# More gathered tokens, a turned value product and a float32 retrieval table in an encoder layer with a product-key expert block

## The chip, the cores and the metric

The kernel runs on one core of one Trainium2 chip. The metric is the device time of one execution in microseconds (us), the median of the runs. PE is TensorE, DVE is VectorE, ACT is ScalarE, POOL is GpSimd, SP is SyncE, which here only issues DMAs.

## What is computed

One encoder layer on 512 tokens of width 2048 in float32. Its last part, the expert block, is what changes:

```python
q = (xt @ w_query).reshape(t, P_HEADS, 2, P_HALF)
s = jnp.einsum('thcd,hcnd->thcn', q, sub_keys)
sv, si = lax.top_k(s, P_TOPK)
cand = sv[:, :, 0, :, None] + sv[:, :, 1, None, :]
cidx = si[:, :, 0, :, None] * N_KEYS + si[:, :, 1, None, :]
top_s, top_j = lax.top_k(cand.reshape(t, P_HEADS, P_TOPK * P_TOPK), P_TOPK)
idx = jnp.take_along_axis(cidx..., top_j, axis=-1)
g = jax.nn.softmax(top_s, axis=-1)
ue = jnp.take(expert_u, idx, axis=0)
ve = jnp.take(expert_v, idx, axis=0)
act = jax.nn.gelu(jnp.einsum('td,thkd->thk', xt, ue), approximate=False) * g
out = h + jnp.einsum('thk,thkd->td', act, ve)
```

There are 16384 experts (128 x 128 keys), 8 heads and 16 experts a head, so each token uses 128 (expert, weight) slots. `expert_u` and `expert_v` are 128 MiB each.

## The kernel before

Float32 products are made of float32r parts: each operand is split into a high and a low part, and `mm3` issues three matmuls (high x high, high x low, low x high) into one PSUM bank. A common stream of 1 MiB weight granules feeds all products: `take` at granule i makes the high part of granule i+2 on ACT (`whi`, L104), the low part of i+1 on DVE (`wlo`, L109) and has SP fetch granule i+4 (`raw`, L89). There are three buffers of each.

The expert block handles tokens in two ways. The 128 tokens of block 0 **gather**: slot by slot, an indirect DMA of POOL fetches 128 rows of 8 KB (one a token), and DVE makes a dot product (L912, with `expert_u`) or adds a weighted row (L1014, with `expert_v`). The other 384 tokens (`SD`) go **dense** over all 16384 experts, in two stages of 128 steps each.

Score stage (`score`): a step takes 128 experts, 16 slices of 128 rows, 48 matmuls of 384 moving tokens with `expert_u` as the stationary side. ACT applies Gelu and writes the 128 x 384 scores to DRAM (`s_d`). Beside it run, in portions that `Paced` hands out four times a step, the choice of experts (`choose`, on DVE, for four blocks of 128 tokens), the gather's dot products, and the **retrieval table**: for each dense token a 128 x 128 matrix of weights over its experts, the product of two one-hot matrices over the 128 slots. `rb` is made by two ACT instructions (L863, L864), `ra` by one on DVE (L872) with high and low part of the weight side by side, one float32r matmul of 256 columns (L847) multiplies them, ACT copies the high half of two tokens (L851) and DVE adds the low half (L856). Sixteen tokens make a `gs` tile, written to `g_d`.

Value stage: in a step i, 256 experts by 1024 output columns; chunks of 8 steps share 1024 experts (4 steps for one half of the columns, 4 for the other). `weigh` multiplies the stored scores with the stored table (L986, in place in `st`) and splits the product into `ath` (ACT, L121) and `atl` (DVE, L122). These are the stationary side; the expert granule moves, 512 columns a matmul, 36 matmuls a step, into 6 of 8 PSUM banks, which DVE adds to `acc` (L1051) after each half chunk. SP loads the table of the next chunk (`gt`, 1.5 MiB) and the scores (`st`); each `st` load is issued one step ahead of its use:

```python
            if j % 2 == 0:
                load_scores(ck + 1, j // 2)
            else:
                weigh(ck + 1, j // 2)
```

Every engine works its instructions in order, so one that waits holds up all behind it.

Of the kernel before, what the change touches and what calls it, by code (L numbers as in the profile page):

```python
# [16 lines left out]
P = 128  # L17
S = 512
D = 2048
# [9 lines left out]
G0 = P  # L29
SD = S - G0  # L30
FH = 258
# [4 lines left out]
def tile_encoder_layer(ctx: ExitStack, tc: tile.TileContext, x, g1, g2, qkg, sg, lv, nd, cs, cc,  # L36
# [18 lines left out]
    g_d = dram.tile([SD // GT, P, NE, GT], F32, name="g_d")  # L55
# [149 lines left out]
    sgs, qkgs, rstd0, lam = few[:, 5:7], few[:, 7:9], few[:, 9:10], few[:, 10:11]  # L205
    idx0 = const.tile([P, P], U32, name="idx0")
    w0 = const.tile([P, P], F32, name="w0")
    dots = const.tile([P, P], F32, name="dots")
    qks = few[:, 11:11 + HEADS + 1]
# [441 lines left out]
    with ExitStack() as st:  # L651
# [32 lines left out]
        nc.vector.tensor_copy(rstd0, rstd[0])  # L684
# [85 lines left out]
    def choose(tb):  # L770
# [58 lines left out]
        if tb == 0:  # L829
            nc.vector.scalar_tensor_tensor(idx0, abf[:, 0].rearrange("p h k -> p (h k)"), float(NE),  # L830
                                           abf[:, 1].rearrange("p h k -> p (h k)"), op0=ALU.mult, op1=ALU.add)
            return
        yield 0.5
        sel = vals[0].rearrange("p (a b) k -> p a (b k)", a=2)
        selw = idxs[0].bitcast(F32R).rearrange("p (a b) k -> p a (b k)", a=2)
# [6 lines left out]
        split(ps[:, 2 * P:3 * P], selw[:, 0], selw[:, 1])  # L842
        late, sums, rbs = [], [], {}

        def place():
            gs, ps, t, ra, rb = late.pop(0)
            nc.tensor.matmul(ps[:, t % 2], rb, ra.rearrange("p a b -> p (a b)"), start=True, stop=True)  # L847
            if t % 2:
                t0 = t % GT - 1
                pair = gs[:, :, t0:t0 + 2].rearrange("p i t -> p t i")  # L850
                nc.scalar.copy(pair, ps[:, :, :P])  # L851
                sums.append((gs, ps, t, pair))

        def add():
            gs, ps, t, pair = sums.pop(0)
            nc.vector.tensor_add(pair, ps[:, :, P:], pair)  # L856
            if t % GT == GT - 1:
                nc.scalar.dma_start(g_d[((tb - 1) * P + t) // GT], gs)

        for t in range(-2, P):  # L860
            if t + 2 < P:
                rbs[t + 2] = rb = pool.tile([P, P], F32R, name="rb", bufs=6)
                nc.scalar.activation(rb, iota, AF.Abs, bias=sel[:, 1, t + 2:t + 3], scale=-1.0)  # L863
                nc.scalar.activation(rb, f32(rb), AF.Relu, bias=unit, scale=-1.0)  # L864
            if t < 0:
                continue
            if t % GT == 0:
                gs = gpool.tile([P, NE, GT], F32, name="gs")
            if t % 2 == 0:
                ps = bank("tr").rearrange("p (t a) -> p t a", t=2)  # L870
            ra = pool.tile([P, 2, P], F32R, name="ra", bufs=4)
            nc.vector.scalar_tensor_tensor(ra, iota[:, None, :].to_broadcast([P, 2, P]), sel[:, 0, t:t + 1],  # L872
                                           f32(selw[:, :, t:t + 1]).to_broadcast([P, 2, P]),
                                           op0=ALU.is_equal, op1=ALU.mult)
            late.append((gs, ps, t, ra, rbs.pop(t)))
            if t % 2:
                if sums:
                    add()
# [5 lines left out]
        while sums:  # L884
            add()

    def begin():
        gb = big.tile([P, D], F32, name="b8")
        nc.scalar.dma_start(hn0, h_d[0])
        nc.scalar.dma_start(gb, bass.AP(tensor=g2r.tensor, offset=g2r.offset, ap=[[0, P], [1, D]]))  # L890
        yield from choose(0)
        nc.vector.scalar_tensor_tensor(hn0, hn0, rstd0, gb, op0=ALU.mult, op1=ALU.mult)
# [5 lines left out]
    def gather_dots():  # L898
        rows = {}

        def fetch_row(s):
            if s < P:
                rows[s] = big.tile([P, D], F32, name="b8")
                nc.gpsimd.indirect_dma_start(out=rows[s], out_offset=None, in_=eu,
                                             in_offset=bass.IndirectOffsetOnAxis(ap=idx0[:, s:s + 1], axis=0))
# [3 lines left out]
        for s in range(P):  # L909
            fetch_row(s + 2)  # L910
            row = rows.pop(s)
            nc.vector.scalar_tensor_tensor(row, row, 1.0, hn0, op0=ALU.mult, op1=ALU.mult,  # L912
                                           accum_out=dots[:, s:s + 1])
# [15 lines left out]
    E0, LAST = 7, NE - 6  # L929
    begin, others = Paced(begin(), 30.5), Paced(others(), 3 * (33.5 + 64 * 1.0))  # L930
    gather = Paced(gather_dots(), float(P))
# [33 lines left out]
    nc.scalar.activation(dots, dots, AF.Gelu)  # L965
    nc.vector.tensor_mul(w0, w0, dots)
    pg.close()
    p6.close()

    pool = pool_of(ctx, "p7")  # L970
    gts, sts, ats = {}, {}, {}

    def load_weights(ck):
        gts[ck] = pool.tile([P, SD // GT, R, GT], F32, name="gt")
        nc.sync.dma_start(gts[ck], g_d[:, :, ck * R:(ck + 1) * R, :].rearrange("c p i t -> p c i t"))

    def load_scores(ck, e2):
        i0 = ck * R + 2 * e2
        sts[ck, e2] = pool.tile([P, 2, SD], F32, name="st", bufs=2)
        nc.sync.dma_start(sts[ck, e2], s_d[i0:i0 + 2].rearrange("e p t -> p e t"))  # L980

    def weigh(ck, e2):
        st = sts.pop((ck, e2))
        for ee in range(2):
            sv = st[:, ee, :].rearrange("p (c t) -> p c t", t=GT)
            nc.vector.tensor_mul(sv, sv, gts[ck][:, :, 2 * e2 + ee, :])  # L986
        h = pool.tile([P, 2, SD], F32R, name=f"ath{e2}", bufs=2)
        l = pool.tile([P, 2, SD], F32R, name=f"atl{e2}", bufs=2)
        split(st, h, l)
        ats[ck, e2] = (h, l)  # L990

    load_weights(0)
    for e in range(LAST, NE):
        score(e, pool, None)
        if e - LAST < R // 2:
            load_scores(0, e - LAST)
        if 0 < e - LAST <= R // 2:
            weigh(0, e - LAST - 1)
# [154 lines left out]
```

## Time and profile before

| | us |
|---|---|
| median of 3 runs (3970.6 to 3976.12) | 3971.14 |
| the profiled execution | 3967.92 |
| its span | 3966.2 |
| score stage, 1751.2 to 2868.9 of the span | 1117.7 |
| value stage, 2868.9 to 3962.2 | 1093.3 |
| from the end of the value stage to the end of the span | 4.0 |

The stages' bounds are the starts of their first matmuls, and the start and end of the last. Starts in a timeline are what sets the pace of PE: its matmuls overlap, so the duration of one is longer than the distance to the next.

### The profile page before, as it was taken

The page shows a single profiled execution, that of the slowest core. Times are in us where ns is not written, and L with a number is a line of the kernel's source. Part 1 is how long each engine was busy: PE and PEld are TensorE (multiplying, and loading weights), DVE is VectorE, ACT ScalarE, POOL GpSimd, SP SyncE. Part 2 cuts the span into 40 slices and gives each one's busy share as a digit, 9 for nine tenths or more (in the row PEclk, how much of TensorE's full clock was granted, in tenths as well). Part 3 has the DMA queues.
Part 4 walks back from the last instruction along what each step waited for, and adds up shares of the span by engine and source line. Part 5 has one row for each costly group of instructions (what it writes and reads, how often), then busy time and mean ns, then how long its engine had stood idle before and what let it go on. Part 6 is the DMA issues. An engine that isn't in the chain of part 4 may idle for free.

```text
span 3966.2 us, 49642 instructions
## 1 busy us (share of the span) xinstructions
PE 3904.3 (98%) x20143; PEld 3459.1 (87%) x20143; DVE 2642.2 (67%) x3884; ACT 1501.0 (38%) x2120; POOL 504.5 (13%) x339
## 2 busy tenths in 40 slices
PE   8999999999999999999999999999999999999999
PEld 6888898888888888889999999999978788787777
DVE  5534555556423424689999888989567787777875
ACT  4322323333322222233675477378422222222221
POOL 0000111111000000001111211211022222222221
PEclk9999999999999999999999999999999999999999
DMA  4334122222333333237888788878788788787885
GB/s 159 112 133 146 64 96 80 80 80 80 107 122 133 135 121 125 98 123 266 299 310 299 286 314 304 307 288 318 245 306 312 283 308 310 286 306 292 310 298 194
DMA packets 209229, 836.65 MB, mean 211 GB/s; under 512 B 15292, under 2 KB 97244, under 8 KB 134876
## 3 DMA queue, kind: packets, MB, share of 16 engines
q1 hardware_dynamic: 147136, 498.11, 35.1%
q0 software_dynamic: 36992, 268.47, 18.1%
q10 hardware_dynamic: 24872, 66.89, 4.4%
q8 instruction: 159, 2.61, 0.3%
q14 instruction: 70, 0.57, 0.0%
HBM read 766.30 MB, written 67.11 MB: 210 GB/s over the span
## 4 chain that ended last, share of the span: by engine, by line
PE 74%; DVE 10%; DMA 8%; issue 5%; ACT 1%; POOL 0%; SPq 0%; DVEq 0%; ACTq 0%; POOLq 0%
PE mm L131 20%; PE mm L133 20%; PE mm L132 20%; DMA st<-s_d 8%; DVE wlo L109 4%; DVE acc L1014 3%; PE vb L132 3%; PE vb L133 3%; PE vb L131 2%; DVE acc L1051 2%; DVE st L986 1%; PE tr L131 1%; PE tr L132 1%; PE tr L133 1%; ACT ath L121 1%
## 5 line engine op out<-in xcount | busy, mean ns | idle before, releaser
L104 ACT CAST whi<-raw 128x2048 fp32r<-128x2048 f32 x395 | 753.8, 1911 | 1004.0 <-PE vb L133 373.1
L131 PE MATMUL mm<-ah,whi 128*128 128x384 f32 (+1 forms) x3072 | 1087.6, 354 | 0.0
L132 PE MATMUL mm<-al,whi 128*128 128x384 f32 (+1 forms) x3072 | 1083.7, 353 | 0.0
L133 PE MATMUL mm<-ah,wlo 128*128 128x384 f32 (+1 forms) x3072 | 1083.6, 353 | 0.0
L109 DVE TENSOR_TENSOR wlo<-raw,whi 128x2048 fp32r<-128x2048 f32 x395 | 901.5, 2285 | 264.0 <-ACT whi L104 264.0
L132 PE MATMUL vb<-wlo,ath 128*128 128x512 f32 x1536 | 602.7, 392 | 33.0 <-DVE wlo L109 33.0
L133 PEld LDWEIGHTS mm<-ah,wlo 128*128 128x128 f32 x3072 | 577.3, 188 | 40.2
L131 PEld LDWEIGHTS mm<-ah,whi 128*128 128x128 f32 x3072 | 577.7, 188 | 39.1 <-issue 0.2
L132 PEld LDWEIGHTS mm<-al,whi 128*128 128x128 f32 x3072 | 577.5, 188 | 39.1
L131 PE MATMUL vb<-whi,ath 128*128 128x512 f32 x1536 | 601.0, 391 | 2.7 <-DVE acc L1051 2.7
L133 PE MATMUL vb<-whi,atl 128*128 128x512 f32 x1536 | 600.8, 391 | 0.0
L131 PE MATMUL mm<-whi,ah 128*128 128x512 f32 (+1 forms) x1408 | 501.8, 356 | 2.9 <-ACT ah L121 2.9
L133 PE MATMUL mm<-whi,al 128*128 128x512 f32 (+1 forms) x1408 | 496.3, 352 | 0.0
L132 PE MATMUL mm<-wlo,ah 128*128 128x512 f32 (+1 forms) x1408 | 495.6, 352 | 0.0
L132 PEld LDWEIGHTS vb<-wlo,ath 128*128 128x128 f32 x1536 | 290.2, 189 | 99.0 <-DVE wlo L109 38.9
L1012 POOL DMA_INDIRECT row<-in_ev_dram,idx x128 | 252.7, 1974 | 859.3 <-DVE acc L1014 743.7
L131 PEld LDWEIGHTS vb<-whi,ath 128*128 128x128 f32 x1536 | 290.2, 189 | 64.7 <-DVE acc L1051 3.9
L133 PEld LDWEIGHTS vb<-whi,atl 128*128 128x128 f32 x1536 | 290.4, 189 | 60.2
L912 DVE SCALAR_TENSOR_TENSOR b<-b,hn 128x2048 f32<-128x2048 f32 x128 | 292.0, 2287 | 13.5 <-DMA b<-in_eu_dram,idx 13.5
L1014 DVE SCALAR_TENSOR_TENSOR acc<-row,w,acc 128x2048 f32<-128x2048 f32 x128 | 300.1, 2344 | 0.3
L133 PEld LDWEIGHTS mm<-whi,al 128*128 128x128 f32 x1408 | 267.2, 190 | 37.3 <-DVE al L122 0.7
L131 PEld LDWEIGHTS mm<-whi,ah 128*128 128x128 f32 x1408 | 267.5, 190 | 36.4 <-ACT ah L121 3.6
(303 smaller groups left out, 3506.0 us busy)
## 6 DMA issues: line engine op xcount, KB each, us to landing
raw<-in_up_dram SPq DMA_DIRECT2D x128, 1024.0 KB, 5.6
raw<-in_ev_dram SPq DMA_DIRECT2D x128, 1024.0 KB, 7.8
raw<-in_wqkv_dram SPq DMA_DIRECT2D x48, 1024.0 KB, 4.8
s_d<-ge ACTq DMA_DIRECT2D x128, 192.0 KB, 4.6
g_d<-gs ACTq DMA_DIRECT2D x24, 1024.0 KB, 9.0
gt<-g_d SPq DMA_DIRECT2D x16, 1536.0 KB, 15.8
st<-s_d SPq DMA_DIRECT2D x64, 384.0 KB, 7.2
raw<-in_wgf_dram SPq DMA_DIRECT2D x16, 1024.0 KB, 4.8
```

The lines of the kernel that those rows point to most:

```text
L104: nc.scalar.copy(his[i], raws[i])
L109: nc.vector.tensor_sub(los[i], raws.pop(i), f32(his[i]))
L121: nc.scalar.copy(hi, src)
L131: nc.tensor.matmul(ps, ah, bh, start=first, stop=False, skip_group_check=shared)
L132: nc.tensor.matmul(ps, ah, bl, start=False, stop=False, skip_group_check=shared)
L133: nc.tensor.matmul(ps, al, bh, start=False, stop=last, skip_group_check=shared)
L912: nc.vector.scalar_tensor_tensor(row, row, 1.0, hn0, op0=ALU.mult, op1=ALU.mult, accum_out=dots[:, s:s + 1])
L986: nc.vector.tensor_mul(sv, sv, gts[ck][:, :, 2 * e2 + ee, :])
L1012: nc.gpsimd.indirect_dma_start(out=row, out_offset=None, in_=ev, in_offset=bass.IndirectOffsetOnAxis(ap=idx1[:, s:s + 1], axis=0))
L1014: nc.vector.scalar_tensor_tensor(acc[0], row, w0[:, s:s + 1], acc[0], op0=ALU.mult, op1=ALU.add)
L1051: nc.vector.tensor_add(acc[tb + 1][:, ds_], banks[tb * 2 + dc], acc[tb + 1][:, ds_])
```

## The change

A second group of tokens is gathered: the first 32 of block 1 (`G2`), so that 160 tokens gather and `SD` is 352. One instruction serves four slots of each of the 32 tokens (4 x 32 partitions), so 32 more indirect DMAs and 32 more DVE instructions in each gather. Their normed rows are read four times from DRAM (`hn_d`), multiplied with the gain and parked in `hg_d`. The table's matmul is float32 with 128 columns, without the split; ACT copies four tokens at a time. `g_d` is laid out by chunk, so that it is written in pieces of 512 B and read contiguously. In the value stage the expert granule is the stationary side and the 352 tokens move; 8 banks fill and are added to a turned sum `accT`. Scores are loaded three uses ahead. After the last step the sums are turned back, added to h (loaded there) and written.

```diff
+G2 = 32
+Q = P // G2
+G0 = P + G2
 SD = S - G0
...
-    g_d = dram.tile([SD // GT, P, NE, GT], F32, name="g_d")
+    g_d = dram.tile([P, NE // R, NG, R, GT], F32, name="g_d")
...
         def place():
             gs, ps, t, ra, rb = late.pop(0)
-            nc.tensor.matmul(ps[:, t % 2], rb, ra.rearrange("p a b -> p (a b)"), start=True, stop=True)
-            if t % 2:
...
-                nc.scalar.copy(pair, ps[:, :, :P])
+            nc.tensor.matmul(ps[:, t % 4], rb, ra, start=True, stop=True)
+            if t % 4 == 3:
+                at = t % GT - 3
+                nc.scalar.copy(gs[:, :, at:at + 4].rearrange("p i t -> p t i"), ps)
...
-            nc.vector.tensor_add(pair, ps[:, :, P:], pair)
...
-            ra = pool.tile([P, 2, P], F32R, name="ra", bufs=4)
-            nc.vector.scalar_tensor_tensor(ra, iota[:, None, :].to_broadcast([P, 2, P]), sel[:, 0, t:t + 1],
+            ra = pool.tile([P, P], F32, name="ra", bufs=5)
+            nc.vector.tensor_scalar(ra, iota, sel[:, 0, t:t + 1], selw[:, t:t + 1],
...
             if t % 2:
...
-                yield 1.0
+                yield 0.5
...
+        nc.vector.tensor_mul(hn0, hn0, gb)
+        hb = big.tile([P, D], F32, name="b8")
+        for r in range(Q):
+            nc.scalar.dma_start(hb[r * G2:(r + 1) * G2], hn_d[P:G0])
+        nc.vector.tensor_mul(hb, hb, gb)
+        nc.scalar.dma_start(hg_d, hb)
...
-    begin, others = Paced(begin(), 30.5), Paced(others(), 3 * (33.5 + 64 * 1.0))
-    gather = Paced(gather_dots(), float(P))
+    begin, others = Paced(begin(), 30.5), Paced(others(), 3 * 33.5 + SD * 0.25)
+    gather = Paced(gather_dots(), P + G2 + 1.0)
...
+    def load_scores(n):
+        if n < len(pairs):
+            sts[n] = pool.tile([P, 2, SD], F32, name="st", bufs=3)
+            nc.sync.dma_start(sts[n], s_d[2 * n:2 * n + 2].rearrange("e p t -> p e t"))
...
+    nc.sync.dma_start(acc0, h_d[0])
+    nc.gpsimd.memset(acc2, 0.0)
...
+    def add_up(ck, half, dt, ps):
+        dst = accT[:, half * 8 + dt, :]
+        if ck == 0:
+            nc.scalar.copy(dst, ps)
+        else:
+            nc.vector.tensor_add(dst, ps, dst)
...
+    shares = [0.8, 0.8, 1.3, 1.0, 1.3, 1.3, 0.8, 0.7]
+    given, total = 0.0, sum(shares) * (NE // R) - 6.0
+    owed, first_use = [], {step_of(n): n for n in range(len(pairs))}
     for i in range(NE):
...
         vh, vl = take(2)
...
+        for job in owed:
+            add_up(*job)
...
+        for dt in range(8):
+            ds_ = slice(dt * P, dt * P + P)
...
+            for ee in range(2):
+                mm3(banks[dt], (vh[:, ee, ds_], vl[:, ee, ds_]), (h[:, ee, :], l[:, ee, :]),
+                    e2 == 0 and ee == 0, e2 == R // 2 - 1 and ee == 1)
+        n = first_use.get(i + 2)
+        if n is not None:
+            weigh(n)
+            load_scores(n + 3)
+        if j == 2 and ck > 0:
+            load_weights(ck + 1)
+        given += shares[j]
+        gather.to(given / total)
+        if e2 == R // 2 - 1:
+            for dt in range(4):
+                add_up(ck, half, dt, banks[dt])
+            owed = [(ck, half, dt, banks[dt]) for dt in range(4, 8)]
...
+    for t0, n in ((P, G2), (G0, P), (G0 + P, P), (G0 + 2 * P, SD - 2 * P)):
+        row = accp.tile([P, D], F32, name="row", bufs=3)
+        nc.sync.dma_start(row[:n], rows_d[t0:t0 + n])
+        for dc in range(4):
...
+            if t0 < G0:
+                nc.tensor.matmul(ps[:n], some, acc2[:, ds_], start=True, stop=True)
             else:
+                for k in range(4):
+                    nc.tensor.transpose(ps[:n, k * P:(k + 1) * P], accT[:, dc * 4 + k, t0 - G0:t0 - G0 + n], ident)
+            nc.vector.tensor_add(row[:n, ds_], ps[:n], row[:n, ds_])
+            nc.sync.dma_start(out[t0:t0 + n, ds_], row[:n, ds_])
```

Three places show how instructions move. First SP's queue in a middle chunk of the value stage, before:

```order
L975 DMA gt<-g_d 128x24x128
L980 DMA st<-s_d 128x2x384
L89 DMA raw<-in_ev_dram 128x2x1024 x2
L980 DMA st<-s_d 128x2x384
L89 DMA raw<-in_ev_dram 128x2x1024 x2
L980 DMA st<-s_d 128x2x384
```

and SP's queue there after the change:

```order
L94 DMA raw<-in_ev_dram 128x2x1024
L1005 DMA gt<-g_d 128x2816
L94 DMA raw<-in_ev_dram 128x2x1024 x4
L1010 DMA st<-s_d 128x2x352
L94 DMA raw<-in_ev_dram 128x2x1024
L1010 DMA st<-s_d 128x2x352
```

The loads are the same in kind, but an `st` load now serves the third use after it, three to seven steps later, where it served the next step.

Second DVE's order around the end of a half chunk in the value stage, before:

```order
L1014 SCALAR_TENSOR_TENSOR acc_24303<-row,w_87,acc_24303 128x2048
L986 TENSOR_TENSOR st<-st,gt 128x384 x2
L122 TENSOR_TENSOR atl_27022<-st,ath_27021 128x768
L1051 TENSOR_TENSOR acc_24304<-vb,acc_24304 128x512 x2
L1051 TENSOR_TENSOR acc_24305<-vb,acc_24305 128x512 x2
L1051 TENSOR_TENSOR acc_24306<-vb,acc_24306 128x512 x2
L109 TENSOR_TENSOR wlo<-raw,whi 128x2048
```

and DVE there after the change:

```order
L1058 SCALAR_TENSOR_TENSOR acc_23814<-row,w_89,acc_23814 128x2048 x2
L1068 TENSOR_TENSOR accT<-vb,accT 128x352 x4
L114 TENSOR_TENSOR wlo<-raw,whi 128x2048
L1068 TENSOR_TENSOR accT<-vb,accT 128x352 x4
L1058 SCALAR_TENSOR_TENSOR acc_23814<-row,w_89,acc_23814 128x2048
```

The half's sums are added in two groups of four with a `wlo` between them, and `weigh` no longer stands at this place in every half.

Third SP's queue at the end of the program, before:

```order
L89 DMA raw<-in_ev_dram 128x2x1024 x5
L1016 DMA out_dram<-acc_24303 128x2048
L1053 DMA out_dram<-acc_24304 128x512 x2
L1053 DMA out_dram<-acc_24305 128x512 x2
L1053 DMA out_dram<-acc_24306 128x512 x2
```

and SP's queue there after the change:

```order
L94 DMA raw<-in_ev_dram 128x2x1024 x5
L1112 DMA row<-h_d 32x2048
L1122 DMA out_dram<-row 32x512 x4
L1112 DMA row<-h_d 128x2048
L1122 DMA out_dram<-row 128x512 x4
L1112 DMA row<-h_d 128x2048
L1122 DMA out_dram<-row 128x512 x4
L1112 DMA row<-h_d 96x2048
L1122 DMA out_dram<-row 96x512 x4
```

Before, only writes stood at the end; now loads of h stand between the writes, each behind the four writes of the tile ahead.

## Rows read from the trace of the kernel before

**Rows 1.** Stage by stage: busy time (instructions) of each engine, granted clock, DMA.
```profile
core 0: us, PE busy (x) PEld busy (x) DVE busy (x) ACT busy (x) POOL busy (x), PEclk, DMA share, GB/s
...
1922.00:2140.50 218.50, 218.24 (x1297) 217.61 (x1296) 196.68 (x265) 171.94 (x357) 31.49 (x28) 1.00 0.83 303
2140.50:2251.00 110.50, 110.50 (x640) 110.47 (x640) 101.30 (x189) 39.12 (x43) 19.06 (x15) 1.00 0.83 300
...
2868.90:3962.20 1093.30, 1057.60 (x4609) 869.13 (x4607) 800.52 (x626) 287.70 (x187) 252.70 (x128) 0.99 0.80 293
```

**Rows 2.** The same view of three stretches without a stall: 256, 384, 512 moving columns.
```profile
409.50:432.50 23.00, 23.00 (x193) 23.00 (x192) 9.13 (x17) 4.88 (x4) 3.99 (x2) 1.00 0.26 93
1809.50:1892.70 83.20, 83.20 (x482) 83.20 (x481) 73.76 (x153) 26.94 (x23) 12.98 (x11) 1.00 0.81 294
2982.50:3031.40 48.90, 48.90 (x217) 40.52 (x216) 32.84 (x26) 13.80 (x9) 11.56 (x6) 1.00 0.84 309
```

**Rows 3.** Who waited for whom in the value stage: us, times, longest.
```profile
DVE st L986 <- DMA st<-s_d: 199.1, 29, 12.3
...
DVE atl L122 <- ACT ath L121: 54.3, 60, 1.1
...
PE vb L132 <- DVE wlo L109: 33.0, 14, 5.7
```

**Rows 4.** PE's timeline at a key match (float32) and at a table product.
```profile
1608.97 1.05 PE L726 MATMUL tr<-b,qT 128*128 128x128 f32 x8
1609.78 0.48 PE L131 MATMUL mm<-ah,whi 128*128 128x512 f32 x1
1610.10 0.40 PE L132 MATMUL mm<-al,whi 128*128 128x512 f32 x1
...
2095.49 0.40 PE L847 MATMUL tr<-ra,rb 128*128 128x256 f32 x2
2095.72 0.34 PE L131 MATMUL mm<-ah,whi 128*128 128x384 f32 x1
```

**Rows 5.** ACT's timeline while the table is made.
```profile
2098.01 0.49 ACT L937 ACTIVATE ge<-mm 128x384 f32<-128x384 f32 x1 [1.29 <-PE mm L133]
2098.53 0.34 ACTq L938 DMA_DIRECT2D s_d<-ge  x1
2098.91 1.92 ACT L104 CAST whi<-raw 128x2048 fp32r<-128x2048 f32 x1 [0.41 <-ACT ge L937]
2100.72 0.40 ACT L863 ACTIVATE rb<-iota,vals 128x128 fp32r<-128x128 f32 x1
...
2102.19 0.58 ACT L851 COPY gs<-tr 128x256 f32<-128x256 f32 x1
2102.57 0.38 ACT L863 ACTIVATE rb<-iota,vals 128x128 fp32r<-128x128 f32 x1
```

**Rows 6.** The chain that ended last, in a stretch of the value stage: start, us, what.
```profile
3045.49 2.47 DVE acc L1051 x4
...
3052.43 2.20 DVE wlo L109
3054.63 2.26 DVE acc L1014
3056.89 0.95 DVE st L986 x2
...
3057.86 0.85 ACT ath L121
```

**Rows 7.** The gathered rows of the value stage: issues, additions, time to landing.
```profile
L1012 POOL DMA_INDIRECT row<-in_ev_dram,idx x128: 939/1897/2933, 2887.4 to 3902.5; - x128
...
DMA to landing us min/median/max: 7.4/10.1/13.4
```

**Rows 8.** DVE's timeline: the last addition; DMA issues of the page, with us to landing.
```profile
3962.39 0.69 DVE L1051 TENSOR_TENSOR acc<-vb,acc 128x512 f32<-128x512 f32 x1 [0.67 <-PE vb L133]
...
raw<-in_wga_dram SPq DMA_DIRECT2D x16, 1024.0 KB, 4.8
```

**Rows 9.** DMA rate in 40 slices of the two stages, score and value.
```profile
GB/s 208 169 299 272 301 334 260 311 299 320 294 323 285 330 284 315 292 318 228 327 294 303 320 289 315 307 310 290 325 249 320 274 306 355 315 252 369 249 265 163
...
GB/s 334 303 328 289 344 235 303 325 297 342 233 302 323 278 339 297 283 316 299 333 268 268 296 277 345 314 270 312 293 330 295 284 318 286 342 269 285 276 234 39
```

**Rows 10.** Weight loads of the value stage: busy us, mean ns of one.
```profile
L132 PEld LDWEIGHTS vb<-wlo,ath 128*128 128x128 f32 x1536 | 290.2, 189 | 99.0 <-DVE wlo L109 38.9
```

More of the change, by code (lines that the diff above doesn't have):

```diff
@@ L28 @@
 GT = 16
-G0 = P
+G2 = 32
+Q = P // G2
+G0 = P + G2
 SD = S - G0
+NG = SD // GT
 FH = 258
@@ L54, in tile_encoder_layer @@
     s_d = dram.tile([NE, P, SD], F32, name="s_d")
-    g_d = dram.tile([SD // GT, P, NE, GT], F32, name="g_d")
+    g_d = dram.tile([P, NE // R, NG, R, GT], F32, name="g_d")
+    hn_d = dram.tile([G0, D], F32, name="hn_d")
+    hg_d = dram.tile([P, D], F32, name="hg_d")
     def bank(tag):
@@ L208, in tile_encoder_layer @@
     dots = const.tile([P, P], F32, name="dots")
+    iw2 = const.tile([P, 2, G2], U32, name="iw2")
+    idx2, w2 = iw2[:, 0], f32(iw2[:, 1])
+    dots2 = const.tile([P, G2], F32, name="dots2")
     qks = few[:, 11:11 + HEADS + 1]
@@ L1022, in tile_encoder_layer @@
         vh, vl = take(2)
-        if i < 4:
-            tb = (i + 1) % NT
-            nc.sync.dma_start(acc[tb], h_d[tb])
+        for job in owed:
+            add_up(*job)
+        owed = []
         if e2 == 0:
-            banks = [vps.tile([P, 512], F32, name="vb") for _ in range(6)]
-        h, l = ats[ck, e2]
-        for tb in range(3):
-            ts_ = slice(tb * P, (tb + 1) * P)
-            for dc in range(2):
-                ds_ = slice(dc * 512, dc * 512 + 512)
-                for ee in range(2):
-                    mm3(banks[tb * 2 + dc], (h[:, ee, ts_], l[:, ee, ts_]), (vh[:, ee, ds_], vl[:, ee, ds_]),
-                        e2 == 0 and ee == 0, e2 == R // 2 - 1 and ee == 1)
@@ L1036, in tile_encoder_layer @@
-        if i == 2:
-            nc.vector.tensor_copy(idx1, idx0)
-        if i >= 4:
-            gather.to((i - 3) / (NE - 8))
-        if ck + 1 < NE // R:
-            if j == 0:
-                load_weights(ck + 1)
-            if j % 2 == 0:
-                load_scores(ck + 1, j // 2)
-            else:
-                weigh(ck + 1, j // 2)
-        if e2 == R // 2 - 1:
-            for tb in range(3):
-                for dc in range(2):
-                    ds_ = slice(half * 1024 + dc * 512, half * 1024 + dc * 512 + 512)
-                    nc.vector.tensor_add(acc[tb + 1][:, ds_], banks[tb * 2 + dc], acc[tb + 1][:, ds_])
-                    if ck == NE // R - 1:
-                        nc.sync.dma_start(out[(tb + 1) * P:(tb + 2) * P, ds_], acc[tb + 1][:, ds_])
@@ L1054, in tile_encoder_layer @@
-    gather.to(1.0)
+            banks = []
+        h, l = ats[ck * 4 + e2]
+        for dt in range(8):
+            ds_ = slice(dt * P, dt * P + P)
+            if e2 == 0:
+                banks.append(vps.tile([P, 512], F32, name="vb")[:, :SD])
+            for ee in range(2):
[5 more added lines that the diff above has]
+            load_scores(n + 3)
@@ new lines, in tile_encoder_layer @@
+        if j == 2 and ck > 0:
[6 more added lines that the diff above has]
+            owed = [(ck, half, dt, banks[dt]) for dt in range(4, 8)]
+    gather.to(1.0)
+    rows_d = h_d.rearrange("n p d -> (n p) d")
+    some = pool.tile([P, G2], F32, name="some")
+    nc.vector.tensor_reduce(some, ident.rearrange("p (r t) -> p t r", r=Q), axis=AX.X, op=ALU.add)
```

146 lines of the change are left out of this document (85 added, 61 removed).

## The prediction

> **What bounds the kernel now.** I read the stages first. In both stages of the expert block PE is busy nearly all the time, at full clock, and DVE for 73 to 92% of it [rows 1]. A busy PE is not yet a PE at its pace, so next I looked at stretches where nothing waits: 192 matmuls of 256 columns take 23.0 us, 480 of 384 take 83.2, 216 of 512 take 48.9 [rows 2]: 119.8, 173.3 and 226.4 ns from start to start. The steps are 53.5 and 53.1 ns for 128 columns, so a matmul costs 0.416 ns a column and some 13 ns that don't depend on its width. At this pace the score stage's 6144 matmuls need 1064.9 us and its 192 pairs of table products 44 (0.23 a pair, [rows 4]); the stage takes 1117.7, so 9 us are stall. The value stage's 4608 matmuls need 1043 of 1093, so 50 are stall. The waits name the cause: PE waits for `wlo`, and DVE, which makes it, stood 199 us waiting for `st` and 54 for ACT's `ath` [rows 3]. With its 800.5 us of work [rows 1] that fills 1054 of 1093 us: DVE has no room to be late. Ahead of the score stage the change only adds 1.25 MB of writes of the normed rows; the query products run on beside them, and without that cover they would cost one transfer, about 5 us [rows 8].
>
> **The change, part by part.**
>
> *Score matmuls.* 352 instead of 384 columns: 173.3 - 32 x 0.416 = 160.0 ns, 6144 times: **-81.9 us**. 256 and 384 columns stand on either side, so little is open.
>
> *Value matmuls.* 48 a step instead of 36, each of 352 columns: 6144 x 160.0 = 983.0 instead of 1043: **-60**. The turned product pays 13 ns a third more often, and wins by 384 against 352 dense tokens.
>
> Against this speaks a rule of the Trainium skill ("Perfetto Trace Analysis", section "Identifying the Most-Contended Engine"): matmul busy time misleads, and the summed time of the weight loads is the better measure of how near TensorE is to its limit. Here it would go from 4608 x 189 ns [rows 10] = 871 us to 6144 x 189 = 1161, more than the stage has now. The trace does not bear it out as a bound: in the stretch of 256 columns 192 loads, 36 us at 189 ns, fit in 23.0 us [rows 2, 10]. As a mechanism it stands among the rivals.
>
> *Table.* Four float32 matmuls of a key match show as eight records [rows 4]. From their start to that of the second matmul behind them pass 1.13 us, of which an ordinary 0.23 is not theirs: 0.90, or 0.226 a matmul and 0.45 a pair. 176 pairs make 79 us, where 192 made 44: **+35**. DVE loses its additions and half of each `ra`.
>
> ACT is close behind. Between table steps it spends 1.47 us on the four activations of a pair (2100.72 to 2102.19) and 0.38 on a copy of 256 columns [rows 5]. The copy of 512 is not in the trace: 0.38 plus 256 columns at 1.82/2048 = 0.61 at least, twice its busy 0.58 at most; I take 0.7, 0.35 a pair. Paced by 0.25 a token, 100.5 units for the choices and 88 for the tables go over 115 steps, so table stretches last 54 steps with 3.28 pairs each: PE 7.68 + 3.28 x 0.45 = 9.16 us a step, ACT 3.28 x 1.82 + 1.82 (`whi`) + 0.90 (Gelu and its write) + 0.16 (`g_d` write, taken like that of the scores) = 8.85. So PE stays ahead by little; I allow 5 us, between none and, at a copy of 1.16, 0.44 x 54 = 24.
>
> In a choice stretch DVE is busy 101.3 of 110.5 us [rows 1]: 14 `wlo` and 14 gather instructions at 2.2 leave 39 for 33.5 units, 1.16 each. Now a step holds 1.64 units (1.9), one `wlo` (2.2) and 1.38 gather instructions (3.1): 7.2 of 7.68. That was 92% and becomes 94, without stalls so far. One wait is new: `hb` is multiplied right after its loads are issued, and behind it stands a `wlo`; a load takes about 5 us [rows 8], so 4 us of PE. The hidden loss when the gather changes to `hg_d` is alike, but a `yield` lies between. Score stage rest: 9 becomes 18, **+9**.
>
> *Value stage stalls.* The `st` wait of 199 us goes: a load is three to seven steps ahead of its use. What DVE does instead in a chunk, by the chain's steps [rows 6]: 8 `wlo` at 2.20, 10 additions of rows at 2.26, 16 of banks at 0.45 (0.62 for 512 columns, between 0.42 in proportion and 0.62), 4 weighings of 0.87 + 0.78 waiting for ACT + 0.87: 57.5 us, at most 60.2. PE needs 8 x 7.68 = 61.4. So DVE fits, at 94 to 98%, with no more than 4 us a chunk to give.
>
> Two places are tight. At the end of a half chunk the second four banks have to be added before PE wants them 3.84 us into the next step, with a `wlo` ahead of them: I take 1.3 us a chunk, 20 in all. And the gather now starts with the stage: the first row is asked for when the score stage's operands are free and POOL has cleared `acc2`, takes 1.9 us to issue and about 10 to land [rows 7], and two additions and a `wlo` follow, about 20 us into the stage; PE wants that `wlo` at 15.4. That is 5 to 6 us once. Together 26 where 50 were: **-24**; bounds 5 (DVE in time everywhere) and 75 (rows late, below).
>
> *The end.* SP issues each load of h behind the four writes of the tile ahead, and these wait for DVE. From PE's last matmul: the sums of the last banks and the four float32 products of the small group take about 4.3 us; then three times a load of 4.8 [rows 8] and four additions of 0.6; then, as now, 3.1 from the last addition (3963.1) to the end of the span: 29 us instead of 4, **+25**. With loads of 2 us it would be +17, with 10.1 us [rows 7] +41.
>
> **Sum.** -81.9 - 60 + 35 + 9 - 24 + 25 = -97. From the profiled execution's 3967.9 (its span and 1.7 around it) that gives 3871; the median of the runs stands 3.2 higher, so **3874 us**.
>
> **Rivals.**
>
> *Rows late, DVE the bound.* Three row buffers turn in landing + addition: at 10.1 us and 2.3 a row every 4.1 us, and 160 rows in 983 us need one every 6.1, in the busiest steps every 4.5. Landings already spread from 7.4 to 13.4 us, and the transfers per us rise by a sixth. At 16.6 us a row comes every 6.3; the gather ends six steps early by plan, so the stage takes 160 x 6.3 + 46 = 1054: 3919. From 17.6 us on the whole gain is gone. For it: DVE's queue has no room; against: only 0.3 us of waiting for rows so far.
>
> *DMA the bound, slower.* Counted from the program, the value stage moves 350 MB (134 of granules, 168 of rows, 23 each of scores and table), the score stage 355. At the rate of now, 293 and 291 GB/s [rows 9], they would last 1195 and 1220 us; with the longer end, 204 + 25 over now, 4200. It decides from below 322 GB/s: (350 + 355) MB in the 2211 us of now less 25. Against it: the rate of now is what PE asks for, and slices reach 345, 355 and 369 [rows 9]; needed are 329 and 347.
>
> The Trainium skill ("DMA: Bandwidth & Descriptors", section "Where 436 GB/s comes from") puts the limit of HBM for a core near 358 GB/s. By it the value stage's 350 MB need 978 us at least, as long as PE does; a slice of 369 says the limit lies a little higher here.
>
> *Weight loads the bound.* 6144 x 189 ns = 1161 us for the value stage and 26 of stall: +178 on my sum, 4052. Against it the stretch above.
>
> *No stall left in the value stage and a short end:* -21 and -8: 3845. For it: every large wait of the value stage's DVE but ACT's goes.
>
> *ACT the bound in the table stretches:* +19, 3893.
>
> **How the numbers follow.** My case 0.60, with 3852 to 3896 as its own range; rows late 0.17; no stall 0.12; ACT 0.05; DMA 0.05; weight loads 0.01. The range from 3838 to 3922 takes in all but the last two and the far end of late rows. Within 0.2% (8 us, about what a measurement can tell) hardly any case falls: faster 0.92, same 0.02, slower 0.06 (DMA, weight loads).
>
> **What the profile would show.** Starts of 160 ns between matmuls of 352 columns in both stages; 0.45 us for a pair of table products; no `st` wait of note on DVE; PE waiting for `wlo` or `accT` at the ends of half chunks; three loads of h, each with DVE idle before it, in an end of about 29 us. I am wrong if DVE waits for rows (late rows), if DMA is busy throughout with PE idle (DMA), or if the distance of matmuls is above 160 ns (loads).

## The result: 4022.6 us, slower by 1.2%

The changed kernel took 4022.59 us (median of 4 runs, 4018.52 to 4027.4), the kernel before 3973.28 beside it (4 runs, 3970.6 to 3976.12): a ratio of 1.0124, 95% interval 1.0107 to 1.0142. I had forecast 3874, from 3838 to 3922, so both the sign and the range are wrong. Of the eight executions of experiment 5 below one took 8428 us; the ratio given there is of the others. The profiled execution has a span of 4017.7 us; all figures of a stage, here and below, come from one profiled execution of each kernel. By stages, with what the terms of the sum would have made of each:

| us | before | forecast | after |
|---|---|---|---|
| up to the score stage | 1751.2 | 1751 | 1779.9 |
| score stage | 1117.7 | 1080 | 1170.5 |
| value stage | 1093.3 | 1009 | 1031.7 |
| end | 4.0 | 29 | 35.5 |

The span is 148 us above the forecast one: 29 ahead of the score stage, 91 in it, 22 in the value stage and 6 at the end. These are the windows of the changed kernel's last three stages, columns as in [rows 1]:

```profile
1779.90:2950.40 1170.50, 1100.21 (x6859) 1087.27 (x6859) 896.42 (x1371) 639.05 (x1065) 285.66 (x165) 0.97 0.84 306
2950.50:3982.20 1031.70, 992.00 (x6145) 986.86 (x6143) 853.10 (x649) 293.30 (x205) 348.69 (x161) 0.99 0.87 333
3982.20:4017.70 35.50, 10.78 (x58) 6.93 (x56) 10.69 (x17) 0.00 (x0) 0.00 (x0) 0.71 0.57 170
```

PE's pace is not what failed. Two stretches of the same view without a stall, one of each stage, answer to [rows 2]:

```profile
2613.20:2689.30 76.10, 76.10 (x477) 76.10 (x477) 66.69 (x61) 26.15 (x22) 28.16 (x13) 1.00 0.95 368
2973.00:3047.00 74.00, 74.00 (x467) 74.00 (x467) 59.33 (x32) 26.62 (x30) 31.42 (x13) 1.00 0.95 367
```

76.1 us for 476 distances are 160 ns, 74.0 for 466 are 159. A pair of table products (four records), on PE's timeline (start, us):

```profile
2829.49 0.61 PE L867 MATMUL tr<-ra,rb 128*128 128x128 f32 x4
2829.86 0.41 PE L136 MATMUL mm<-ah,whi 128*128 128x352 f32 x1
2830.10 0.32 PE L137 MATMUL mm<-al,whi 128*128 128x352 f32 x1
```

What failed is how often such a stretch breaks off. Here is first the kernel before's wait for gathered rows in the score stage, then the chief waits of the changed kernel there (who waited for whom: us, times, longest):

```profile
DVE b L912 <- DMA b<-in_eu_dram,idx: 13.5, 7, 4.3
```
```profile
DVE b L933 <- DMA b<-in_eu_dram,idx: 72.7, 36, 8.1
ACT whi L109 <- issue: 38.2, 10, 7.3
...
PE tr L867 <- ACT rb L879: 24.8, 25, 3.9
PE mm L138 <- DVE wlo L114: 24.1, 10, 10.3
...
PE tr L859 <- DVE idxs L838: 18.3, 3, 6.9
```

Three things are to be seen here: DVE waits for gathered rows; ACT stands ten times, up to 7.3 us, with nothing to wait for that the profile knows ("issue"); and PE waits for the one and the other. ACT's timeline at the longest of these, and PE's beside it:

```profile
2830.07 0.53 ACTq L872 DMA_DIRECT2D g_d<-gs  x1
...
2832.12 0.45 ACT L958 ACTIVATE ge<-mm 128x352 f32<-128x352 f32 x1
2832.60 7.14 ACTq L959 DMA_DIRECT2D s_d<-ge  x1
2839.84 1.90 ACT L109 CAST whi<-raw 128x2048 fp32r<-128x2048 f32 x1 [7.27 <-issue]
2841.64 0.40 ACT L878 ACTIVATE rb<-iota,vals 128x128 f32<-128x128 f32 x1
```
```profile
2838.41 0.32 PE L138 MATMUL mm<-ah,wlo 128*128 128x352 f32 x1
2842.52 0.49 PE L867 MATMUL tr<-ra,rb 128*128 128x128 f32 x2 [3.79 <-ACT rb L879]
...
2844.41 0.49 PE L138 MATMUL mm<-ah,wlo 128*128 128x352 f32 x1
2844.71 0.49 PE L136 MATMUL mm<-ah,whi 128*128 128x352 f32 x1
```

The first issue of a score tile behind a write of g_d took 7.14 us instead of the 0.34 of [rows 5]; `whi` and `rb` stood behind it on ACT, and PE waited 3.79 us for `rb`. After the wait its matmuls start 293 ns apart instead of 160. That is the lower of its two clocks, 1.2 GHz: the granted clock, in the last column but two of a window, is 0.50 for 2.5 us of them, and 0.64 in the mean of 4.5 us, at whose end the clock is full again:

```profile
2844.00:2846.50 2.50, 2.50 (x11) 2.50 (x10) 2.50 (x4) 2.40 (x8) 0.00 (x0) 0.50 0.56 140
2843.50:2848.00 4.50, 4.50 (x22) 4.50 (x23) 4.50 (x6) 4.37 (x11) 0.95 (x1) 0.64 0.66 225
```

So a stall costs more than its length: of the score stage's matmuls 130 start some 293 ns apart, 17 us more than at the full clock. In the value stage DVE's groups (busy, mean ns | idle before them, and what ended it), and PE's wait at the ends of half chunks:

```profile
L1058 DVE SCALAR_TENSOR_TENSOR acc<-row,w,acc 128x2048 f32<-128x2048 f32 x128 | 300.5, 2348 | 64.0 <-DMA row<-in_ev_dram,idx 63.1
...
L1058 DVE SCALAR_TENSOR_TENSOR acc<-row,iw,acc 128x2048 f32<-128x2048 f32 x32 | 75.1, 2348 | 20.1 <-DMA row<-in_ev_dram,iw 19.9
L127 DVE TENSOR_TENSOR atl<-st,ath 128x704 fp32r<-128x704 f32 x62 | 55.4, 893 | 69.5 <-ACT ath L126 69.5
```
```profile
PE vb L136 <- DVE accT L1068: 35.9, 15, 8.0
```

The wait for `st`, 199 us in [rows 3], is gone, and 83 us for rows have come. At the end, as forecast, stand three waits for loads of h:

```profile
DVE row L1121 <- DMA row<-h_d: 19.7, 3, 7.1
```

### The profile page after: what moved, and what is told of

The parts are those of the page before. It is cut to its first block, busy times and chain, and to the rows that moved or that the text cites. A ratio compares the mean times of both kernels' runs of the same rounds, so it can differ in the third digit from the quotient of the medians.

```text
span 4017.7 us, 53473 instructions
## 1 busy us (share of the span) xinstructions
PE 3862.4 (96%) x22055; PEld 3561.6 (89%) x22055; DVE 2619.6 (65%) x3759; ACT 1465.7 (36%) x1966; POOL 723.9 (18%) x408
## 5 line engine op out<-in xcount | busy, mean ns | idle before, releaser
L138 PE MATMUL mm<-ah,wlo 128*128 128x352 f32 (+1 forms) x3072 | 1074.1, 350 | 24.1 <-DVE wlo L114 24.1
L136 PE MATMUL mm<-ah,whi 128*128 128x352 f32 (+1 forms) x3072 | 1092.2, 356 | 0.0
L137 PE MATMUL mm<-al,whi 128*128 128x352 f32 (+1 forms) x3072 | 1073.3, 349 | 0.0
L136 PE MATMUL vb<-ath,whi 128*128 128x352 f32 x2048 | 665.8, 325 | 35.9 <-DVE accT L1068 35.9
L138 PE MATMUL vb<-ath,wlo 128*128 128x352 f32 x2048 | 661.3, 323 | 3.8 <-DVE wlo L114 3.8
L137 PE MATMUL vb<-atl,whi 128*128 128x352 f32 x2048 | 660.1, 322 | 0.0
L136 PEld LDWEIGHTS vb<-ath,whi 128*128 128x128 f32 x2048 | 387.0, 189 | 40.7 <-issue 31.9
L933 DVE SCALAR_TENSOR_TENSOR b<-b,hn 128x2048 f32<-128x2048 f32 x160 | 363.6, 2286 | 84.6 <-DMA b<-in_eu_dram,idx 72.7
L138 PEld LDWEIGHTS vb<-ath,wlo 128*128 128x128 f32 x2048 | 387.6, 189 | 4.0 <-DVE wlo L114 4.0
L137 PEld LDWEIGHTS vb<-atl,whi 128*128 128x128 f32 x2048 | 388.2, 190 | 0.0
L921 POOL DMA_INDIRECT b<-in_eu_dram,idx x128 | 223.8, 1748 | 835.0 <-DVE b L933 386.6
## 6 DMA issues: line engine op xcount, KB each, us to landing
gt<-g_d SPq DMA_DIRECT2D x16, 1408.0 KB, 14.9
```

The costliest lines, as they stand in the source:

```text
L136: nc.tensor.matmul(ps, ah, bh, start=first, stop=False, skip_group_check=shared)
L137: nc.tensor.matmul(ps, ah, bl, start=False, stop=False, skip_group_check=shared)
L138: nc.tensor.matmul(ps, al, bh, start=False, stop=last, skip_group_check=shared)
L933: nc.vector.scalar_tensor_tensor(row, row, 1.0, hrow, op0=ALU.mult, op1=ALU.mult, accum_out=jobs[s][1])
```

## The experiments

All were timed beside the kernel before; "the changed kernel" is the one above.

**1. Placement.** The code ahead of the score stage differs only by the writes of the normed rows and one small copy that is gone, but the two new tensors among the constants, 384 bytes a partition, move every buffer behind them: `raw`, `whi` and `wlo` lie 384 bytes further up, while the activations, at the other end of SBUF, stay. One run moves them to 512, and one moves those of the kernel before to 384.

```
+    const.tile([P, 32], F32, name="pad")      # changed kernel
+    const.tile([P, 96], F32, name="pad")      # kernel before; rb: bufs 6 -> 5
```

> The changed kernel with 128 unused bytes a partition behind its constants, so that the granule buffers raw, whi and wlo lie 512 bytes from their place in the kernel before instead of 384. Theory, placement: the 28.7 us that the changed kernel has lost by the time its score stage starts (1779.9 instead of 1751.2) come from where its buffers lie in SBUF, since the code up to there is otherwise the same and a matmul of 512 columns takes 232 instead of 227 ns. Then the score stage starts at 1751 to 1754 us, matmuls of 512 columns are back at 227 ns, and the whole takes about 3994. Rival, other cause (the program's length, HBM addresses of larger tensors): the score stage starts at 1778 to 1782 and the whole stays at 4020 to 4025.

> The kernel before with 384 unused bytes a partition behind its constants (and five buffers for rb instead of six, to make room), so that its granule buffers lie where those of the changed kernel lie. Theory, placement: the score stage starts at 1776 to 1782 us instead of 1751.2, matmuls of 512 columns take 232 ns, and the whole takes 4000 or more. Rival, other cause: nothing moves; 1751 and 3970 to 3976.

The first took 3996.44 us (ratio to the kernel before 1.0061, 1.0045 to 1.0078, where the changed kernel had 1.0124), the second 3985.84 (1.0038, 1.0023 to 1.0052). The score stage starts at 1753.1 and at 1778.6. Here is the same window, 1100 to 1500 us, in which there are only matmuls of 512 columns at full clock and no stall, of the kernel before, the changed one, the first run and the second:

```profile
1100.00:1500.00 400.00, 400.00 (x1767) 331.20 (x1765) 127.51 (x85) 98.73 (x75) 0.00 (x0) 1.00 0.35 128
```
```profile
1100.00:1500.00 400.00, 400.00 (x1723) 324.30 (x1722) 126.84 (x84) 95.90 (x72) 0.00 (x0) 1.00 0.35 126
```
```profile
1100.00:1500.00 400.00, 400.00 (x1766) 331.34 (x1765) 127.49 (x85) 98.01 (x73) 0.00 (x0) 1.00 0.35 129
```
```profile
1100.00:1500.00 400.00, 400.00 (x1723) 324.29 (x1722) 126.79 (x84) 95.89 (x72) 0.00 (x0) 1.00 0.34 125
```

In 400 us PE starts 1767, 1723, 1766 and 1723 matmuls: 227 or 232 ns apart, by the place of the buffers alone. For the pace and for the start of the score stage the theory was right in both directions. The 28.7 us lost ahead of the score stage are this, but for some 2 us. The whole of the second missed its 4000 or more: its score stage became 10 us longer (1128.2; matmuls of 384 columns start 175 ns apart instead of 173), but its value stage 13 us shorter (1080.2), which I had not foreseen and no run explains.

In the score stage of the padded run the starts are not 160 ns apart but 158 in some stretches and 167 in others (median 166), changing over only where a stall or table products break the row; the stage keeps 1169.2 us. No one of the places tried is best for every shape.

**2. Layout of g_d.** One write in 128 pieces of 8 KB again.

```
-    g_d = dram.tile([P, NE // R, NG, R, GT], F32, name="g_d")
+    g_d = dram.tile([NG, P, NE, GT], F32, name="g_d")
...
+                nc.scalar.dma_start(g_d[(tb * P + t - G0) // GT], gs)
...
+            nc.sync.dma_start(gts[ck], g_d[:, :, ck * R:(ck + 1) * R, :].rearrange("c p i t -> p c i t"))
```

> The changed kernel with the granule tensor g_d laid out by blocks of 16 tokens as before, so that a write takes 128 pieces of 8 KB instead of 2048 of 512 bytes, and the load in the value stage takes the small pieces instead. Theory, blocked queue: the 15 issues of scores (line 959) that took 1.1 to 7.1 us, each right behind such a write, fall to the ordinary 0.33; the nine waits of PE for ACT's rb in the score stage go, and with them part of the stretches at half clock; the score stage takes 1130 to 1150 instead of 1170.6, the whole 3982 to 4002. Rival, ACT is late for its own work (copies of 512 columns at 1.09 us): the issues get short but PE's waits stay, and the score stage keeps 1165 to 1175.

**3. Who issues it.** The new layout is kept, and SyncE issues the write.

```
-                nc.scalar.dma_start(g_d[:, :, (tb * P + t - G0) // GT]...
+                nc.sync.dma_start(g_d[:, :, (tb * P + t - G0) // GT]...
```

> The changed kernel with one word altered: SyncE issues the writes of the granule tensor g_d, in the new layout of 2048 pieces, and no longer ACT. Theory, blocked queue: what costs in the score stage is that the next transfer issued on the queue of such a write waits for up to 7 us, and on ACT copies and activations stand behind it. On SyncE only loads of raw granules stand behind it, which are asked for four granules ahead. So the 15 long issues on ACT go, PE's waits for rb (24.8 us in the score stage) go, and the stage falls as with the layout by blocks of tokens, from 1170.6 to 1125 to 1140; some issues of raw on SyncE take 1 to 7 us. The value stage keeps its large loads and about 1032 us. Whole about 3978. Rival, the small pieces themselves cost (they take the transfers' time from rows and granules): the stage keeps 1160 or more although ACT is free.

The layout by blocks gave 3957.02 us, a ratio of 0.9963 (0.9951 to 0.9974), with a score stage of 1127.7; SyncE gave 3980.29, 1.0018 (1.0008 to 1.0028), with a score stage of 1123.3. The issues of scores in the changed kernel and with the layout by blocks (ns, smallest, median, largest), and of the granules on SyncE's queue in run 3:

```profile
L959 ACTq DMA_DIRECT2D s_d<-ge x128: 321/326/7142, 1789.7 to 2951.1; - x128
```
```profile
L958 ACTq DMA_DIRECT2D s_d<-ge x128: 326/326/934, 1786.5 to 2905.2; - x128
```
```profile
L94 SPq DMA_DIRECT2D raw<-in_up_dram x123: 327/328/4365, 1787.0 to 2863.1; - x123
```

In the changed kernel 15 issues were over 1 us, 47 us above the ordinary one in all. With SyncE ACT has none, its longest is 0.36, and 22 issues of `raw` on SyncE are long instead, 50 us above the ordinary, behind which nothing urgent stands. The delay follows the queue of the write, and it goes with the pieces; the pieces as such cost nothing that shows here (the rival of run 3). PE's waits for `rb`, 24.8 us above, are gone with them (none in run 2, 0.2 us in run 3), so ACT being late with its own work, the rival of run 2, is out. Both runs put this step at 43 to 47 us of the score stage, somewhat more than I had expected. The value stage took 1020 us in run 2 and 1042 in run 3, where I had expected no change from 1032; by the one, the whole of run 2 is shorter than the 3982 to 4002 that I had named. In the first run of experiment 1 and in run 4, whose edits lie outside it, it took 1039 and 1041, so a difference of 10 us in this stage tells nothing. The Trainium skill ("DMA: Bandwidth & Descriptors", section "Issuing engines are not separate DMA queues") says that a choice of issuing engine saves no more than the time of the initiation on its sequencer, and that this is usually small relative to the DMA itself. The trace agrees with the first; it is not small here, up to 7.14 us an issue and 47 us in all.

**4. A third row buffer.** The searches on `tail` of all later tiles come first, so that its buffer is free for rows.

```
...
         for tb in range(1, NT):
+            yield from tails(tb)     # the four best() that choose(tb) began with
+        for tb in range(1, NT):
             yield from choose(tb)
```

> The changed kernel with the best-sixteen searches on the four tail blocks of all three later token tiles first, so that the buffer of the tail is free for a third row from about the tenth step of the gather and not only from 2557 us. Theory, rows late for want of a buffer: DVE's waits for gathered rows in the score stage fall from 72.7 us to under 25, the three waits of 5 to 7 us of PE at the transposes of the choices (line 859) get under 2 us, and the score stage takes 1140 to 1158 us instead of 1170.6, the whole 3992 to 4010. Rival, rows come late because of the transfers themselves: DVE's waits stay above 50 us and the stage within 5 us of 1170.

3996.68 us (ratio 1.0063, 1.0041 to 1.0084), score stage 1139.1. DVE's wait for the rows, beside the 72.7 above:

```profile
DVE b L939 <- DMA b<-in_eu_dram,idx: 27.8, 12, 8.4
```

Rows were late for want of a buffer. A miss in part: 27.8 is a little above the 25 I had named, and of the three waits at the transposes one is left, of 8 us. That one never was a wait for late rows. In the changed kernel DVE and PE stand there so:

```profile
2693.29 2.29 DVE L933 SCALAR_TENSOR_TENSOR b<-b,hn 128x2048 f32<-128x2048 f32 x1 [11.67 <-DMA hn<-hg_d]
...
2696.41 0.47 PE L859 MATMUL tr<-ident,idxs 128*128 128x128 f32 x1 [6.48 <-DVE idxs L838]
```

The load of `hg_d`, issued some 10 us before, holds up DVE where the gather changes to the second group, and `idxs` stands behind it. No experiment moves this load: with all edits of run 7 DVE still waits 10 to 11 us for it, and PE 2 to 4.

**5. hb, four row buffers, h ahead.** Three edits in three stages.

```
+        hb = gpool.tile([P, NE, GT], F32, name="gs").rearrange("p a b -> p (a b)")
+        for r in range(Q):
+            nc.scalar.dma_start(hb[r * G2:(r + 1) * G2], hn_d[P:G0])
         yield from choose(0)
...
-        rows[s] = accp.tile([P, D], F32, name="row", bufs=3)
+        rows[s] = accp.tile([P, D], F32, name="row", bufs=4)
-            fetch_row(s + 2)
+            fetch_row(s + 3)
...
+    for t0, n in ((P, G2), (G0, P), (G0 + P, P), (G0 + 2 * P, SD - 2 * P)):
+        row = acc0 if t0 == G0 + 2 * P else accp.tile([P, D], F32, name="row", bufs=4)
+        nc.sync.dma_start(row[:n], rows_d[t0:t0 + n])
+        ends.append(row)
     for job in owed:
```

> The changed kernel with three edits that touch different stages, read each in its own stretch. (1) hb is loaded with hn0 into a free gs buffer when the score stage begins, not when it is needed. Theory, late load: DVE's wait of 3.3 us for it goes, the first row's buffer is free at once, and the stall of 10.6 us of PE 70 us into the score stage falls below 4. Rival: the stall comes from the first gathered row itself and keeps 7 or more. (2) Four buffers of gathered rows in the value stage and rows asked for one further ahead (and five buffers instead of six for ath and atl). Theory, latency: DVE's waits for rows, 83 us there now, fall below 25, PE's stall in the value stage from 43 to under 25, the stage from 1032 to about 1014. Rival, DVE has no room anyway: the waits go but PE's stall stays within 5 of 43; or rows come at the rate of the transfers, and the waits stay. (3) The four loads of h at the end are issued ahead of the output writes. Theory: the three waits of 5.8 to 7.2 us go and the end falls from 35.5 to 15 to 19. Rival: the output's writes, which take SP 2.1 to 2.9 us each to issue, set the end, and it keeps 28 or more. Whole by the theories 3980 to 3988.

3957.86 us, ratio 0.9968 (0.9954 to 0.9982). Its stages, score, value and end:

```profile
1777.60:2933.20 1155.60, 1094.20 (x6860) 1081.07 (x6859) 896.61 (x1371) 638.82 (x1065) 278.68 (x165) 0.98 0.86 310
2933.20:3936.60 1003.40, 989.18 (x6145) 986.87 (x6144) 852.82 (x649) 292.85 (x205) 357.30 (x161) 0.99 0.89 346
3936.60:3953.10 16.50, 9.29 (x59) 6.06 (x57) 10.41 (x17) 0.00 (x0) 0.00 (x0) 0.92 0.60 192
```

DVE's two waits around the late `hb` in the changed kernel, for its loads and then for the first gathered row:

```profile
1836.78 2.29 DVE L906 TENSOR_TENSOR b<-b,b 128x2048 f32<-128x2048 f32 x1 [3.29 <-DMA b<-hn_d]
...
1851.11 2.29 DVE L933 SCALAR_TENSOR_TENSOR b<-b,hn 128x2048 f32<-128x2048 f32 x1 [8.13 <-DMA b<-in_eu_dram,idx]
```

The first is gone and the second fell to 6.7. PE's stall of 10.6 us became 5.5, between the theory's 4 and the rival's 7; the stage lost 15. In the value stage PE's wait for `accT` fell from 35.9 to 10.5 us and DVE's for rows from 83 to 11, and the stage from 1031.7 to 1003.4, more than forecast: the rows were late for latency, and neither DVE's work nor the transfers' rate kept the stage there. The end fell by 19, as expected; a single write to the output takes SyncE some 0.33 us to issue, so the 2.1 to 2.9 us of the rival are those of four. The whole is 22 us below my 3980, half of it in the value stage.

**6. All together, with the layout by blocks**, and 128, no, or 64 unused bytes.

> All together: 128 unused bytes behind the constants, the granule tensor by blocks of 16 tokens, the tail blocks' searches first, hb loaded early, four row buffers in the value stage, loads of h ahead of the end's writes. If the causes are separate, their gains add: 4022.6 less 26 (placement, up to the score stage), 62 (layout), 21 (tails, half of what was measured, since layout may hold part of it), 10 (hb), 18 (rows) and 18 (end) gives 3868, with 3855 to 3885 as the range, and the end of the case against the kernel before is a ratio of about 0.974. Rival, the gains overlap, because a stall that is taken away in one place comes back in the next: 3895 or more.

> All together, but without the 128 unused bytes. Theory, placement acts only ahead of the score stage: 26 us more than with them, all of them before the score stage starts (1777 instead of 1751). Rival, placement acts in the score stage too (there the matmuls with 128 bytes more stood 158 or 167 ns apart, without them 160): the score stage is shorter here than with the padding by up to 25 us, and the whole differs by less than 10.

> All together with 64 unused bytes instead of 128, to see whether a placement between the two gives both good paces. If the pace depends on the distance of the buffers modulo 128 or more, 512-column matmuls lie between 227 and 232 ns or beyond, and the score stage's at neither 160 nor 158 and 167; if only multiples of 128 bytes matter, the starts equal those of one of the two others.

3914.76, 3902.71 and 3918.76 us: ratios 0.9844, 0.9829 and 0.9874, each within 0.003. The rival of the first came: 3895 or more. The score stages fell as hoped, to 1093, 1085 and 1083 us, but the value stages took 1050, 1028 and 1052 instead of the 1003 of run 5. Without the bytes the score stage starts 26 us later than with 128, as the theory had it, but it is 8 us shorter and the value stage 23, so the whole is 12 us less. Neither the theory nor the rival had the value stage's share. With 64 bytes the score stage starts at 1763.6, with starts 231 ns apart for 512 columns: a third pace; but the score stage's starts have a median of 160 ns, as without the bytes.

**7. All together, with the new layout, issued by SyncE.** Its loads are the large pieces again; without and with 64 unused bytes.

> All edits together, with the new layout of g_d issued by SyncE instead of the layout by blocks of tokens. Theory: the layout by blocks gained in the score stage and lost in the value stage, where its loads of 2816 small pieces stand beside the rows and granules (value stage 1027.6 with it, 1003.4 with the new layout and four row buffers). Then here the score stage takes 1080 to 1095 and the value stage 1000 to 1010; score start 1777 to 1780, end 16.5, the whole 3875 to 3890. Rival, the value stage's difference comes from how the two stages stand to each other and not from the layout: it takes 1020 or more.

> The same with 64 unused bytes behind the constants. With 64 the stages ahead of the score stage took 1763.6 instead of 1779.5 and the score stage the same. Theory, placement is separate from the rest: 16 us less than without the bytes, 3860 to 3875, and the best of all kernels. Rival: the value stage gives it back, as it did with the layout by blocks (1052 instead of 1027.6): the same as without the bytes or more.

3880.18 us (ratio 0.9758, 0.9742 to 0.9774) and 3864.38 (0.9724, 0.9705 to 0.9744), the best of all. Its four stages:

```profile
0.00:1763.00 1763.00, 1742.04 (x8997) 1468.98 (x8998) 858.93 (x1724) 533.11 (x696) 89.33 (x83) 1.00 0.30 109
1763.00:2844.10 1081.10, 1068.49 (x6861) 1066.58 (x6860) 893.11 (x1371) 638.94 (x1066) 285.59 (x165) 1.00 0.90 331
2844.10:3849.60 1005.50, 989.64 (x6144) 986.95 (x6143) 852.72 (x649) 292.84 (x205) 354.25 (x161) 0.99 0.89 345
3849.60:3865.90 16.30, 9.26 (x59) 6.04 (x57) 10.41 (x17) 0.00 (x0) 0.00 (x0) 0.91 0.60 194
```

The value stage is back at 1002 and 1005.5, so with four row buffers the layout by blocks did cost it 26 and 47 us (with three, in run 2, it had cost nothing that shows). How is less sure. The issues of the page show a load of granules landing in 20.7 us (median) with the layout of run 2, and in 14.9 in the changed kernel:

```profile
gt<-g_d SPq DMA_DIRECT2D x16, 1408.0 KB, 20.7
```
```profile
gt<-g_d SPq DMA_DIRECT2D x16, 1408.0 KB, 14.9
```

The traces show the held queue of run 3 here too, now on SyncE. These are the issues of granules in the value stage, of the second kernel of experiment 6 (by blocks) and of the first one here, and ACT's waits for granules in both:

```profile
L94 SPq DMA_DIRECT2D raw<-in_ev_dram x124: 367/368/15497, 2865.9 to 3852.3; - x124
...
ACT whi L109 <- DMA raw<-in_ev_dram: 281.9, 45, 14.2
```
```profile
L94 SPq DMA_DIRECT2D raw<-in_ev_dram x123: 367/368/373, 2883.2 to 3823.9; - x123
...
ACT whi L109 <- DMA raw<-in_ev_dram: 181.7, 29, 10.3
```

By blocks a load of `gt` has 2816 pieces of 512 bytes, and all 16 issues right behind one took 3.5 to 15.5 us. But in run 2 they took 3.6 to 13.0 and cost nothing that shows, so that these holds are the 26 and 47 us is likely, but not shown.

## Why the prediction was wrong, step by step

- *Score matmuls, -81.9, and value matmuls, -60.* Right: 160 and 159 ns apart. Weight loads did not become the bound.
- *Table, +35.* Right at 0.45 us a pair: from 2829.49 to the start of the second matmul behind it, 2830.10, are 0.61 us, less one ordinary 0.16.
- *"Ahead of the score stage the change only adds 1.25 MB of writes of the normed rows".* Wrong: +28.7 us, all but some 2 of them by placement. I looked at what the code does there and not at where its operands lie (run 1).
- *Score stage rest, +9.* This step failed most. The stage took 1170.5 - 983 - 79 = 108 us beside its matmuls where I had 18. Four of its parts were mis-sized. "0.16 (`g_d` write, taken like that of the scores)": the write takes ACT 0.53, and the issue behind it up to 7.14; with the lost clock 47 us (run 3). The trace of the kernel before held this price already: its loads of `gt` have 3072 pieces of 512 bytes, and of the 16 issues of `st` right behind one 15 took SyncE 6.2 to 9.1 us (line below). How much of the 199 us of waiting for `st` was this, no run separates. "That was 92% and becomes 94, without stalls so far": I counted DVE's work and not its rows. One of the three buffers of 8 KB is held by `tail` until the last choice, so rows come through two, and 160 rows now pass in the 117 steps that 128 had: DVE waits 72.7 us, and the third buffer gave 31 back (run 4). "So 4 us of PE" for the late `hb`: the first row also wants its buffer, and PE stood 10.6 + 3.5 us; the early load gave 15 back (run 5). "The hidden loss when the gather changes to `hg_d` is alike, but a `yield` lies between": put at nothing, it made DVE wait 11.7 us and PE 6.5 (run 4). The first three of these parts, removed one by one, gave 47 + 31 + 15 = 93; removed together, 1170.5 - 1084.6 = 86. The copy of 512 columns took ACT 1.07 us, near the upper of my bounds, but once the queue was free PE hardly waited for ACT (runs 2 and 3).

```profile
L980 SPq DMA_DIRECT2D st<-s_d x60: 366/463/9080, 2867.3 to 3881.1; - x60
```

- *Value stage stalls, -24.* The stage kept 49 us beside its matmuls where I had 26. The `st` wait went and the turn of `accT` at the half chunks came, both as described, but the rival "rows late" was there in part: 83 us of DVE's waiting at a landing (median 10.6) close to the old 10.1. DVE's work with its wait for `ath` came out as I had it, (853.1 + 69.5) / 16 = 57.7 us a chunk; I had called its room 0 to 4 us and yet priced a row that is late at nothing in the sum. One more buffer gave 28 us (run 5).
- *The end, +25.* The mechanism was right, its size was not: DVE waited 5.8 to 7.2 us for each load where the sum had 4.8, of which the loads themselves took 5.3 to 6.6 and the rest lay between DVE's last addition and SyncE's issue: +31.5.
- *DMA the bound.* Not so: 333 GB/s in the value stage of the changed kernel with PE waiting for DVE, and 345 once those waits are all but gone (run 7). The Trainium skill ("DMA: Bandwidth & Descriptors", section "Where 436 GB/s comes from") puts the limit near 358 GB/s for a core. The trace does not agree: the two stretches without a stall shown above moved 368 and 367 GB/s over 76 and 74 us, with PE at its pace.

With all these edits the kernel's span (run 7, 64 bytes) is 3865.9 where my sum had 3869: partly luck, since it pays 12 us ahead of the score stage and saves 13 at the end.

## What to carry to other kernels

When a change adds a tensor to a pool that others stand behind, compare the distance of unchanged matmuls in an unchanged stage first; a few hundred bytes were worth some 27 us here. Cost a DMA that is cut into many pieces by what stands behind it on the queue that issues it, and choose that queue by who can afford to wait. Look for that price in the trace you have: here it stood in the issues of `st`. Where a gather runs faster than before, count its buffers and who still holds them: where DVE had no more than 4 us a chunk to give, late rows stopped PE, and the longer stops cost clock as well.

## What was not expected of the hardware

- The distance of matmuls depends on where the buffers of granules lie beside the activations: 227, 232 and 231 ns for 512 columns at 0 (or 512), 384 and 448 bytes more than before, and 119.9, 118.6 and 114.4 for 256. By the Trainium skill ("SBUF — State Buffer", section "A bandwidth-pool intuition that's wrong") the weight loads have a read port of their own; which part of the machine makes the difference no run here shows.
- At one place (512 bytes) the 352-column matmuls had two steady paces, 158 and 167 ns, and changed over only where a stall or table products came between.
- An issue of a DMA right behind one of 2048 pieces of 512 bytes took up to 7.14 us of the issuing engine, and behind a load of 2816 such pieces up to 15.5; behind one of 128 pieces of 8 KB it took at most 0.93.
- In the score stage 130 matmuls ran at half the clock, following stalls of 2 to 10 us.
